# Twelve projections of a hybrid layer as seven products of quarters, in a stage of their own

## The chip, the cores and the metric

The kernel runs on one core of one Trainium2 chip. The metric is the device time of one execution in microseconds (us). The core has a matrix engine (TensorE, PE in the profile, with its weight loads as PEld), three engines for elementwise work (VectorE: DVE, ScalarE: ACT, GpSimd: POOL) and SyncE (SP), which here issues nearly all DMA transfers. Each engine works through its own queue in order and waits on semaphores for the others. On-chip memory (SBUF) has 128 partitions; TensorE writes its results to eight banks of PSUM, each of 512 float32 columns.

## The reference

One decoder layer on 1024 tokens of width 1024, with 256 memory tokens. Cut to what matters here:

```python
h = rmsnorm(x, ln1)
z = h @ w_in                       # one wide projection, split into:
ml_qk, ml_v, ml_o, ml_i, ml_f, fx_q, fx_k, fx_v, fx_f = split(z)
ml_qk = silu(causal_conv(ml_qk, conv_w, conv_b))     # 4 taps along the tokens
mh = mlstm_chunkwise(mq, mk, mv, ml_i, log_sigmoid(ml_f + b))   # 4 heads of 128
ml_out = rmsnorm_per_head(mh) * ml_norm * sigmoid(ml_o)         # ml_o: the output gates
fx_out = forgetting_attention(fx_q, fx_k, fx_v, log_sigmoid(fx_f + b))  # 8 heads of 64
x = x + concat(ml_out, fx_out) @ w_out
x = x + cross_attention(rmsnorm(x), rmsnorm(mem), ...)          # 4 heads of 256
x = x + relu(rmsnorm(x) @ w_ff1) ** 2 @ w_ff2
return rmsnorm(x, ln_f)
```

ml_o (output gates), fx_q (forgetting queries) and fx_k (forgetting keys) are each 512 columns wide, four tiles of 128: twelve tiles that read nothing but h.

## The kernel before

Every float32 matrix product is made of three matmuls. `split` writes a high part (ScalarE, rounded to the matmul's own float32 form) and a low part (the rest, VectorE); `mm3` (lines 190 to 194) multiplies low by high, high by low and high by high into one PSUM bank. `weights` loads a 128x1024 weight tile into one of two raw buffers (wr) and splits it into one of three pairs (wh, wl). `proj` makes a tile of 128 columns for both halves of 512 tokens, with eight contraction tiles: 48 matmuls of 512 columns.

Instructions are written in program order and then put into each engine's queue ahead of time: what is ready goes first, and among the ready the one earlier in the program. So a projection written later can be placed between the steps of a chain written earlier. Where the body stands under `in_order`, the written order is kept on each engine. Buffers are named by tag with a fixed count: act (7 tiles of 128x4096), w4 (5 of 128x1024), z4 (2 of 128x1027), r_a to r_y (one or two of 128x512 each). An allocation waits until a buffer of its tag is free.

The stages in order:

- The inputs arrive, are squared for the norm, scaled by the gain ln1 and split into h (four act tiles: two halves of tokens, high and low). The norm's factor per token is applied to results later: rcol has it by token in columns, row in a row over all partitions.
- `token_major` (line 503) makes values with tokens on the partitions, in matmuls of 256 columns. The first half of the mLSTM values is made while the inputs arrive (`first_values`), the second by `token_major(a["w_mv"], ...)` (line 689). `mv_sink` (line 321) keeps all of them in two act tiles. Between its tiles lie the making of row (`row_first`) and `gate_rows` (line 464): the forget gates' running sums by scans on VectorE.
- `ml_project(hd)` (line 668), for each of four mLSTM heads: `conv_silu` for the key (projection, four taps on VectorE, tanh on ScalarE, split), `fx_project(0, hd)` (a forgetting query tile, scaled, split, stored to DRAM as fqk), `carried` (the state that the first half of tokens hands to the second), `conv_silu` for the query, `fx_project(1, hd)` (a key tile), `carry`, and the output gate's tile. `ml_head(hd)` (line 578) computes the scores, their decay (ScalarE, GpSimd's mask, VectorE), their products with the values, the denominators and the normalized result, in pieces; `closing` is the last piece of a head (or, ahead of head 0, the gate columns and the preparing of the memory tokens), taken up between the steps of the next projection.
- Forgetting attention. `fx_load` reads queries and keys into two stacks, one step of loading per slot (`fx_step`, from a list `coming`). Thirteen slots of scores go ahead (the lead), then `token_major(a["w_fv"], ...)` (line 1090) makes the forgetting values, then 96 slots each transpose, split and multiply a piece of the probabilities. Each slot also gets some filler: units from a list (line 961), first the keys and values of the cross-attention (`key_unit`, `value_unit`, four heads), then the tiles of the output projection over the first five contraction tiles (`out_unit`). `RATE` (line 1101) sets how much filler a slot takes: 3.6, where three matmuls of 512 columns count 3.0. `extra` lists the loads of the operands of `out_unit`.
- The rest of the output projection, cross-attention, and the MLP. The MLP's first product, and most of its second, is made by seven products of quarters in place of eight (`Pair`, line 1393; `left_up`, line 1253, makes the combined weights: four subtractions and additions on GpSimd).

## Time and profile before

| | before |
|---|---|
| time, median of 3 runs | 1513.89 us (1513.47 to 1515.79) |
| profiled execution: span from first to last instruction | 1510.9 us |
| TensorE busy, matmuls | 1498.5 us (99%), 7708 |
| VectorE busy | 1097.5 us (73%) |
| ScalarE busy | 717.5 us (47%) |
| GpSimd busy | 450.6 us (30%) |
| DRAM traffic | 288.33 MB, mean 191 GB/s |
| granted TensorE clock | 0.998 |

For the profiled execution the profile gives its span; the time of an execution also holds what lies before the first and after the last instruction. In a row of the groups of instructions, the line is that of the kernel (often a helper's: L192 to L194 are the three matmuls of `mm3`, L138 and L139 the two parts of a `split`), then engine, operation, result and operands with their shapes and the count; after the bar, busy time, mean of one in ns, and idle time of the engine just before them with what ended it. Names of buffers stand without their numbers, m is the bank m2. Matmuls are pipelined: one starts before the one ahead of it has ended, so that the busy time of a matmul is longer than its distance to the next.

### The profile page before, as it was taken

Reading aid. Unit: us, or ns where it says so; the run is one execution under the profiler, and the core shown is the slowest. Engines: PE = TensorE matmul, PEld = TensorE weight load, DVE = VectorE, ACT = ScalarE, POOL = GpSimd, SP = SyncE. Lnnn points to the kernel's source line nnn. Section 1 sums busy time; section 2 is a strip of 40 time slices with the busy share of each in tenths; the row PEclk is TensorE's granted clock in tenths of the full one; section 3 lists DMA queues with packets and bytes.
Section 4 is the critical chain, followed back from the end, with each engine's and each line's share of the span. In section 5 each row is a group of like instructions: output and inputs, shape, how many; then the busy total and the mean of one; then the engine's idle time right before and its main releaser. Section 6 shows DMA issues by size and latency. Waiting matters only on the chain.

```text
span 1510.9 us, 21868 instructions
## 1 busy us (share of the span) xinstructions
PE 1498.5 (99%) x7708; PEld 1259.5 (83%) x7708; DVE 1097.5 (73%) x1743; ACT 717.5 (47%) x1347; POOL 450.6 (30%) x529
## 2 busy tenths in 40 slices
PE   9999999999999999999999999999999999999997
PEld 8988888889999888888888888888888888888887
DVE  7676676665799875844457988888887788777765
ACT  7343343334788773534444556565656332222134
POOL 0003030413466551001110033344433644343312
PEclk9999999999999999999999999999999999999999
DMA  5332333436889768533334446867766865555623
GB/s 209 117 114 91 115 100 127 129 130 169 279 253 270 218 199 291 198 123 119 119 119 133 154 136 237 281 244 265 272 243 235 352 258 221 223 223 223 251 84 112
DMA packets 114258, 288.33 MB, mean 191 GB/s; under 512 B 12882, under 2 KB 23436, under 8 KB 108516
## 3 DMA queue, kind: packets, MB, share of 16 engines
q1 hardware_dynamic: 113860, 286.83, 56.0%
q8 instruction: 60, 0.98, 0.3%
q14 instruction: 50, 0.41, 0.1%
q10 hardware_dynamic: 288, 0.11, 0.0%
HBM read 194.36 MB, written 92.53 MB: 190 GB/s over the span
## 4 chain that ended last, share of the span: by engine, by line
PE 98%; issue 0%; DVE 0%; DMA 0%; POOL 0%; ACT 0%; POOLq 0%; ACTq 0%; DVEq 0%
PE tp L194 9%; PE tp L193 9%; PE tp L192 9%; PE sc L192 7%; PE sc L194 7%; PE sc L193 7%; PE m L192 6%; PE m L194 6%; PE m L193 6%; PE mm L192 6%; PE mm L193 6%; PE mm L194 6%; PE ov L813 2%; PE ov L192 2%; PE ov L193 2%; PE ov L194 2%
## 5 line engine op out<-in xcount | busy, mean ns | idle before, releaser
L194 PE MATMUL tp<-act,wh 128*128 128x512 f32 (+1 forms) x456 | 178.5, 392 | 0.0
L192 PE MATMUL tp<-act,wl 128*128 128x512 f32 (+1 forms) x456 | 178.5, 392 | 0.0
L193 PE MATMUL tp<-act,wh 128*128 128x512 f32 (+1 forms) x456 | 178.5, 391 | 0.0
L138 ACT ACTIVATE wh<-wr 128x1024 fp32r<-128x1024 f32 (+3 forms) x96 | 92.7, 966 | 95.9 <-PE tp L194 36.6
L139 DVE TENSOR_TENSOR wl<-wr,wh 128x1024 fp32r<-128x1024 f32 (+3 forms) x96 | 113.9, 1187 | 14.5 <-ACT wh L138 14.4
L193 PE MATMUL mm<-act,wh 128*128 128x512 f32 (+1 forms) x320 | 122.6, 383 | 0.0
L192 PE MATMUL mm<-act,wl 128*128 128x512 f32 (+1 forms) x320 | 122.6, 383 | 0.0
L194 PE MATMUL mm<-act,wh 128*128 128x512 f32 (+1 forms) x320 | 122.3, 382 | 0.0
L192 PE MATMUL m<-act,wl 128*128 128x512 f32 (+1 forms) x312 | 119.5, 383 | 0.0
L193 PE MATMUL m<-act,wh 128*128 128x512 f32 (+1 forms) x312 | 118.9, 381 | 0.0
L194 PE MATMUL m<-act,wh 128*128 128x512 f32 (+1 forms) x312 | 118.8, 381 | 0.0
L192 PE MATMUL sc<-act,wl 128*128 128x512 f32 (+1 forms) x268 | 103.8, 387 | 0.0
L193 PE MATMUL sc<-act,wh 128*128 128x512 f32 (+1 forms) x268 | 103.7, 387 | 0.0
L194 PE MATMUL sc<-act,wh 128*128 128x512 f32 (+1 forms) x268 | 103.6, 387 | 0.0
L194 PEld LDWEIGHTS tp<-act,wh 128*128 128x128 f32 x456 | 85.7, 188 | 19.5
L193 PEld LDWEIGHTS tp<-act,wh 128*128 128x128 f32 x456 | 85.8, 188 | 19.0
L192 PEld LDWEIGHTS tp<-act,wl 128*128 128x128 f32 x456 | 85.7, 188 | 19.0
L1491 POOL TENSOR_TENSOR z<-wr 128x256 f32<-128x256 f32 x56 | 50.4, 921 | 147.6 <-DMA wr<-w_ff2q 140.8
L138 ACT ACTIVATE w<-wr 128x768 fp32r<-128x768 f32 (+2 forms) x31 | 25.5, 825 | 133.7 <-PE tp L194 69.2
L138 ACT ACTIVATE wh<-z 128x1024 fp32r<-128x1024 f32 (+2 forms) x55 | 52.5, 956 | 65.0 <-POOL z L1491 28.8
L139 DVE TENSOR_TENSOR wl<-z,wh 128x1024 fp32r<-128x1024 f32 (+2 forms) x55 | 65.9, 1198 | 10.1 <-ACT wh L138 10.1
L194 PEld LDWEIGHTS mm<-act,wh 128*128 128x128 f32 x320 | 60.2, 188 | 12.5
(673 smaller groups left out, 4207.9 us busy)
## 6 DMA issues: line engine op xcount, KB each, us to landing
act<-right SPq DMA_DIRECT2D x35, 1024.0 KB
right<-r_d SPq DMA_DIRECT2D x70, 256.0 KB
right<-w SPq DMA_DIRECT2D x56, 256.0 KB
wr<-w_ff2q SPq DMA_DIRECT2D x28, 512.0 KB
act<-fqk SPq DMA_DIRECT2D x48, 256.0 KB
wr<-w_in SPq DMA_DIRECT2D x20, 512.0 KB
wr<-w_ff SPq DMA_DIRECT2D x20, 512.0 KB
fqk<-r_p SPq DMA_DIRECT2D x32, 256.0 KB
```

The costliest lines, as they stand in the source:

```text
L138: s.activation(hi, src, AF.Copy)
L139: return v.tensor_tensor(out=lo, in0=src, in1=hi.bitcast(F32), op=ALU.subtract)
L192: nc.tensor.matmul(ps, w[1], x[0], start=first, stop=False, skip_group_check=more)
L193: nc.tensor.matmul(ps, w[0], x[1], start=False, stop=False, skip_group_check=more)
L194: nc.tensor.matmul(ps, w[0], x[0], start=False, stop=last, skip_group_check=more)
L813: nc.tensor.matmul(self.ov[:, c0:], self.fv[:, self.j], t[:, c0:], start=self.j == 0 and t is self.p[1], stop=self.last and t is self.p[0])
L1491: g.tensor_tensor(out=o, in0=x, in1=y, op=op)
```

## The change

The twelve tiles leave the heads and get a stage of their own ahead of the heads, between the mLSTM values and `ml_project(0)`. They are joined in six couples: gates 0 and 1, then query and key tile n for n from 0 to 3, then gates 2 and 3. A couple is a product of 256 columns by 1024 contraction by 1024 tokens; each factor is cut into quarters, and seven products of combined quarters give the four quarters of the result.

- The combined quarters of the inputs are made from x scaled by ln1 (VectorE and GpSimd) and split. One of them takes the place of half of h's second half, which is saved to DRAM before (h12d) and read back in the last couple.
- The combined quarters of the weights are made on GpSimd, as in the MLP.
- Partial sums are added by VectorE out of PSUM; ScalarE copies one of seven products.
- Gates go through tanh and to DRAM (ogd); each head reads its own back. Queries and keys go to fqk as before.
- The mLSTM values go to DRAM (mvd) instead of staying in two act tiles; each head reads its own into one tile. The second half of the values is made in the order of tokens 4 to 7, then 0 to 3.
- The weights of `conv_silu` have their low part made by GpSimd, and its first tap is made by ScalarE.
- The forgetting values are made behind heads 0 and 1, one half each. Half of the cross-attention's keys and values (heads 0 and 1) leaves the filler: two key tiles behind head 2, the rest between the lead and the slots of forgetting attention.
- In the slots, a second list (`behind`) is loaded from when `coming` is empty; `RATE` is 3.4.
- The memory tokens are prepared during the new stage.

The core of the diff:

```diff
     def mv_sink(t, c, ps):
-        o = mv[c][:, t].rearrange("p (h e c) -> p h e c", h=2, e=2)
+        o = rotate("d", "e").bitcast(F32R).rearrange("p (h e c) -> p h e c", h=2, e=2)
         split(o[:, :, 0], o[:, :, 1], ps.rearrange("p (h c) -> p h c", h=2), rcol[:, t : t + 1])
+        load(mvd[2 * c : 2 * c + 2, :, t].rearrange("h p c -> p h c"), o.bitcast(F32).rearrange("p h e c -> p h (e c)"))
...
-    steps, cum, rel, run = (t[:GW] for t in quarters())
-    on = w4((GW, T))
+    steps, cum, rel, run = (w4((GW, T)) for _ in range(4))
+    on = z4()[:GW, :T]
...
     def conv_silu(n, hi, lo):
-        w = weights(a["w_in"][n])
+        w = weights(a["w_in"][n], by=g)
...
-        v.tensor_scalar(out=y, in0=z[:, 0:T], scalar1=vec[:, cw : cw + 1], scalar2=..., op0=ALU.mult, op1=ALU.add)
+        s.activation(y, z[:, 0:T], AF.Identity, scale=vec[:, cw : cw + 1], bias=...)
...
     def ml_project(hd):
...
+        mv_load(hd)
         yk = conv_silu(MLH + hd, *k)
         next(closing, None)
-        fx_project(0, hd)
-        next(closing, None)
         state = carried(hd, yk)
         next(closing, None)
         yq = conv_silu(hd, *q)
-        fx_project(1, hd)
-        sums = carry(hd, q, yq, *state)
-        og = w4()
-        for _, hf, ps in proj(weights(a["w_in"][8 + hd]), h, 1):
...
+        next(closing, None)
+        return q, k, *carry(hd, q, yq, *state)
...
+    def first_parts():
+        for e in range(2):
+            cut_part(5, x11, e)
+
+    def third_part():
+        for e in range(2):
+            combine(x12, x11, e, v, x11)
+        for e in range(2):
+            combine(x22, x12, e, g, x12)
+
+    def other_parts():
+        for e in range(2):
+            combine(x22, x11, e, v, x11)
+        for e in range(2):
+            cut_part(6, x11, e)
+        for e in range(2):
+            cut_part(7, x12, e)
...
+    def fourth_part():
+        fourth.extend(w4() for _ in range(2))
+        for e in range(2):
+            combine(x21, x11, e, g, fourth)
...
+    couples = [(gate_sink(0), gate_sink(1))] + [(fx_sink(0, n), fx_sink(1, n)) for n in range(4)] + [(gate_sink(2), gate_sink(3))]
+    NC_ = len(couples)
+    seven_jobs = []
+    for p_ in range(NC_):
+        seven_jobs += [(p_, 1), (p_, 5), (p_, 2)] + ([(p_ - 1, 4)] if p_ else []) + [(p_, 6), (p_, 3), (p_, 7)]
+    seven_jobs.append((NC_ - 1, 4))
...
+        if group == 0:
+            rs = [z4()[:, :1024] if p_ % 2 else sb("wr", [P, 1024], 2) for _ in range(2)]
...
+            for o, x, y, op in ((s3, a11, a21, ALU.subtract), (a21, a21, a22, ALU.add), (a22, a22, s3, ALU.subtract), (a12, a12, a22, ALU.subtract)):
+                g.tensor_tensor(out=o, in0=x, in1=y, op=op)
...
+    def seventh(p_, i):
...
+        if i in (1, 5, 6):
+            u[at_] = bank()
+        ps = u[at_]
+        l, r = lefts_.pop((p_, i)), RIGHT[i]
+        for k in range(4):
+            mm3(ps, both(l, lambda t: t[:, k]), both(r, lambda t: t[:, k]), i in (1, 5, 6) and k == 0, k == 3, True)
...
-    token_major(a["w_mv"], mv_sink, (1,), {2: row_first, 5: gate_rows}, other)
+    token_major(a["w_mv"], mv_sink, (1,), {2: between_2, 4: between_4, 5: gate_rows}, other, (4, 5, 6, 7, 0, 1, 2, 3))
+    turn[0] = 0
+    memory = mem_prepare()
+    for at, (p_, i) in enumerate(seven_jobs):
+        left_ahead(at)
+        if at == 0:
+            other_parts()
+        if at == 2:
+            gate_cols()
+        if at == 3:
+            fourth_part()
+        if at == 5:
+            fourth_cut()
+        if at in (12, 16, 20, 24):
+            next(memory, None)
+        seventh(p_, i)
...
     for hd in range(MLH):
         closing = ml_head(hd, *ready)
         next(closing)
+        if hd < 2:
+            token_major(a["w_fv"], fv_sink, (hd,))
+        if hd == 2:
+            next(extra_work)
         if hd < MLH - 1:
             ready = ml_project(hd + 1)
...
-    for n in range(XH):
+    for n in range(2, XH):
         units += [key_unit(2 * n), value_unit(n), key_unit(2 * n + 1)]
...
-    token_major(a["w_fv"], fv_sink, between={4: lambda: next(closing, None)})
...
+    next(extra_work)
+    next(closing, None)
+    for _ in extra_work:
+        pass
...
-    RATE, DELAY = 3.6, 3
+    RATE, DELAY = 3.4, 3
```

`x11`, `x21` are the lower and upper half of the contraction for the first half of the tokens, `x12`, `x22` for the second. `between_2` makes row and the third combination, `between_4` the cuts of product 5 and the first weights; `left_ahead` makes the weights of a product five products ahead of it.

More of the change, by code (lines that the diff above doesn't have):

```diff
@@ L186, in weight_parts @@
         lo = sb("wl", [P, 1024], 3, F32R)[:, :n]
-        split(hi, lo, raw)
+        split(hi, lo, raw, by=by)
         return hi, lo
@@ new lines, in combine, with cut_part @@
+    def combine(x, y, e, by, out_=None):
+        x, y = (flat2(t, c + 2 * e) for t, c in (x, y))
+        o = flat2(out_[0], out_[1] + 2 * e) if type(out_) is tuple else out_[e]
+        by.tensor_tensor(out=o, in0=x, in1=y, op=ALU.subtract)
+    def cut_part(i, x, e, by=v):
+        if i not in RIGHT:
+            t = act()
+            RIGHT[i] = t[:, lower], t[:, upper]
+        split(*both(RIGHT[i], lambda t: flat2(t, 2 * e)), flat2(x[0], x[1] + 2 * e) if type(x) is tuple else x[e], by=by)
```

258 lines of the change are left out of this document (193 added, 65 removed).

## Prediction

> **What bounds the kernel now.** I read the page first, then the waits of TensorE, then the busy time stage by stage, then the timeline of TensorE inside one projection.
>
> ```profile
> span 1510.9 us, 21868 instructions
> PE 1498.5 (99%) x7708; PEld 1259.5 (83%) x7708; DVE 1097.5 (73%) x1743; ACT 717.5 (47%) x1347; POOL 450.6 (30%) x529
> PE 98%; issue 0%; DVE 0%; DMA 0%; POOL 0%; ACT 0%; POOLq 0%; ACTq 0%; DVEq 0%
> ```
>
> The chain that ended last is TensorE for 98% of the span. The waits of TensorE, longest first, hold nothing else of size:
>
> ```profile
> PE ov L228 <- DVE c_r L220: 1.7, 1, 1.7
> PE mm L192 <- DVE act L142: 1.4, 1, 1.4
> PE ov L118 <- DVE r_y L115: 1.2, 1, 1.2
> ```
>
> No wait is longer than 1.7 us. So a matmul taken out is time taken out, one for one, as long as TensorE always finds another whose operands are there. The stages (columns: stretch, length, busy time with instruction count for PE, PEld, DVE, ACT, POOL, then granted clock, DMA share, GB/s):
>
> ```profile
> 57.00:335.00 278.00, 278.00 (x1362) 231.09 (x1361) 189.43 (x286) 103.24 (x167) 48.53 (x62) 1.00 0.36 113
> 335.00:391.00 56.00, 56.00 (x455) 54.31 (x454) 30.64 (x75) 25.05 (x63) 21.89 (x28) 1.00 0.71 207
> 391.00:545.00 154.00, 152.89 (x1078) 140.19 (x1076) 136.68 (x334) 123.70 (x348) 89.22 (x150) 1.00 0.81 243
> 905.00:1410.00 505.00, 505.00 (x2166) 406.85 (x2165) 403.63 (x489) 230.75 (x338) 207.73 (x175) 1.00 0.69 251
> 57.00:67.00 10.00, 10.00 (x62) 8.48 (x61) 9.96 (x10) 3.16 (x5) 0.00 (x0) 1.00 0.23 61
> ```
>
> The rows are: the mLSTM heads with the projections that are to move (57 to 335), the forgetting values and the lead of the scores (335 to 391), forgetting attention, the MLP's products of quarters, and the ten microseconds in which the gate rows are made. TensorE is full in all of them at clock 1.00.
>
> **What a matmul costs.** The page's mean of about 390 ns for one matmul is not its price, because matmuls overlap. The timeline inside one projection gives the pitch:
>
> ```profile
> 59.84 0.40 PE L192 MATMUL tp<-act,wl 128*128 128x512 f32 x1
> ...
> 65.20 0.40 PE L194 MATMUL tp<-act,wh 128*128 128x512 f32 x1
> ...
> 330.28 0.28 PE L192 MATMUL tp<-wh,act 128*128 128x256 f32 x1
> ...
> 333.11 0.28 PE L192 MATMUL mm<-wh,act 128*128 128x256 f32 x1
> ```
>
> From 59.84 to 65.20 lie 23 steps: 0.233 us for 512 columns. From 330.28 to 333.11 lie 24 steps of 256 columns: 0.118 us.
>
> **The products removed.** Before, each of the twelve moved column tiles (four output gates, four query and four key tiles) takes two halves of eight contraction tiles with three matmuls: 48, in all 576. After, each of six couples takes seven products of four contraction tiles with three matmuls: 84, in all 504. 72 matmuls of 512 columns go: 72 x 0.233 = 16.8 us. (With the mean of 392 ns in the group's row below it would be 28 us, which is the trap of this profile.) The Trainium skill, "TensorE: Matmul & The Clock Gate", section "Back-to-back issue gap", gives columns / 2.4 + 2.5 ns; by it a matmul of 512 columns would cost 0.216 us and the saving would be 15.5 us. The trace's 0.233 decides.
>
> ```profile
> L194 PE MATMUL tp<-act,wh 128*128 128x512 f32 (+1 forms) x456 | 178.5, 392 | 0.0
> ```
>
> The forgetting values, the mLSTM projections and the cross-attention keys and values keep their matmuls; they only change place. TensorE's own work falls by 16.8 us and by nothing else.
>
> **The steady run of the new stage.** A couple lasts 84 x 0.233 = 19.6 us of TensorE. VectorE's and GpSimd's rows for its pieces:
>
> ```profile
> L139 DVE TENSOR_TENSOR wl<-wr,wh 128x1024 fp32r<-128x1024 f32 x22 | 26.7, 1215 | 0.0
> L653 DVE SCALAR_TENSOR_TENSOR r_p<-tp,row 128x512 f32<-128x512 f32 x8 | 5.5, 686 | 4.8 <-DMA fqk<-r_p 3.5 <-PE tp L194 1.3
> L139 DVE TENSOR_TENSOR r_p<-r_p,r_p 128x512 fp32r<-128x512 f32 x16 | 12.1, 755 | 3.4 <-ACT r_p L138 3.2
> L1234 POOL TENSOR_TENSOR r_e<-z,z 128x512 f32<-128x512 f32 x7 | 10.8, 1540 | 134.5 <-DMA z<-w_ff 131.4 <-DVE w L1234 3.0
> L1273 POOL TENSOR_TENSOR wr<-wr 128x512 f32<-128x512 f32 x7 | 13.7, 1962 | 0.5
> ```
>
> VectorE per couple: weight splits of 3.5 tiles of 1024 columns, 4.3 us; five additions out of PSUM and four scalings by the token factor, 9 x 0.69 = 6.2; four low parts, 3.0: 13.5 of 19.6 us. GpSimd: four combinations of weights, near 4 x 1.7 = 6.8 us. The MLP stage already runs this scheme with VectorE at 403.6 of 505 us (80%) and GpSimd at 41%, and TensorE loses nothing there; the new stage asks 69% and 35%. I cost the steady run at nothing; were its cover gone, VectorE would set the pace only from 19.6 us per couple.
>
> DRAM carries more: mLSTM values, gates and a saved half of the inputs go out and back, some 16.8 MB (4.2, 2.1 and 2.1 MB, each twice). Spread over 57 to 335 that adds 60 GB/s to the 113 of its row, 173 in all; forgetting attention runs at 243 with TensorE full. SyncE's queue gets the stores of values and gates ahead of later weight loads; a store waits for its sink there, and the weights behind it wait too. The MLP stage queues its stores and loads the same way without loss, so nothing, with 3 us as the bad end.
>
> **The start of the new stage.** Here buffers and VectorE decide. The first couple needs four combined quarters of the inputs. Quarter product 5 is cut into the old second half as soon as the reordered value projection has left it, product 6 goes into the one free activation buffer. Product 7 needs an eighth: it must wait until the fourth combination (GpSimd) has read the first input tile. That combination writes two w4 tiles, and of the five, four hold the gate rows until these are done; the row 57 to 67 shows VectorE at 9.96 of 10 us with just that work (67 us). Then two halves on GpSimd at about 2 x 1.54 each (6 us) and the two cuts, 1.2 us each with ScalarE's part ahead (4 us): about 77 to 79 us. Product 7 is sixth in line, due at 57 + 5 x 2.8 = 71 us. Until then three products of the second couple can pass (8.4 us), if their weights are in. The second couple's raw weights want both z4 buffers, one of which holds the row of ones until the gate rows are done. So the term lies between 0 and 11 us; I take 4, since part of the late supply is passed over.
>
> **The heads without their company.** Before, the head stage mixes the 576 matmuls (134 us) among the heads' own chains. After, heads 0 and 1 get the forgetting values instead (384 x 0.118 = 45.3 us), head 2 two key tiles (5.7 us), the end the other three pieces (17 us). VectorE is relieved as well: the splits of the conv weights go to GpSimd and the first conv tap to ScalarE.
>
> ```profile
> L683 DVE TENSOR_TENSOR w<-tp,row 128x512 f32<-128x512 f32 x4 | 2.7, 684 | 0.0
> L142 DVE SCALAR_TENSOR_TENSOR r_c<-tp,rcol,r_c 128x256 fp32r<-128x256 f32 x3 | 1.5, 484 | 5.5 <-ACT r_c L141 5.5
> L475 DVE TENSOR_TENSOR_SCAN act<-w,act 12x1024 f32<-12x1024 f32 x1 | 2.3, 2278 | 2.3 <-ACT act L470 2.3
> L142 DVE SCALAR_TENSOR_TENSOR w<-act,w 12x1024 fp32r<-12x1024 f32 x2 | 2.4, 1208 | 0.7 <-DMA decay<-w 0.7
> L761 DVE TENSOR_REDUCE c_mx<-sc 128x1 f32<-128x512 f32 x5 | 3.4, 683 | 0.3 <-PE sc L734 0.3
> L525 DVE TENSOR_SCALAR z<-z,vec 128x1024 f32<-128x1024 f32 x8 | 7.2, 906 | 0.2
> L527 DVE SCALAR_TENSOR_TENSOR z<-z,vec,z 128x1024 f32<-128x1024 f32 x24 | 32.3, 1345 | 0.2
> L530 DVE SCALAR_TENSOR_TENSOR z<-z,z 128x1024 f32<-128x1024 f32 x8 | 10.2, 1280 | 1.9 <-ACT z L529 1.9
> L529 ACT ACTIVATE z<-z 128x1024 f32<-128x1024 f32 x8 | 8.5, 1060 | 23.7 <-DVE z L527 23.7
> L994 POOL TENSOR_TENSOR wl<-wr,wh 128x256 fp32r<-128x256 f32 x32 | 26.4, 846 | 5.2 <-ACT wh L988 3.7 <-issue 1.3 <-POOL act L778 0.2
> ```
>
> VectorE from 57 to 391 has 189.4 + 30.6 = 220 us. Out go the weight splits 26.7, L653's 16 operations at 0.69 (11), their low parts 12.1, the gates' 8 at L683's 0.68 (5.5), the taps 7.2: 62 us. The gate rows and decays (two scans, four smaller operations, two decays: 10 to 12) stay with the start. Taking off the values' sinks (16 x 0.48 and four splits, 12.6) and the lead's maxima (13 of at most 0.68, 8 with their small ones), the four heads keep about 125, 31 each. TensorE in the same stretch: 334 - 134 - 45 - 6 for the lead's scores - 3 for the end of the values projection = 146, 36 per head. So heads 0 and 1 stay rich in TensorE work (36 + 22.7 against 31 + 6). The tail, heads 2 and 3 with the three pieces and the lead, has 73 + 22.7 + 6 = 102 us of TensorE against 62 + 15 + 8 = 85 us of VectorE (15: eight weight splits and four keys' and four values' small ones), with perhaps 10 more left over from head 1: 83% to 93%. The nearest row is forgetting attention, VectorE at 136.7 of 154 us (89%), where TensorE is idle for 1.1 us; but that stretch has its order written out and small pieces to fill with, and the tail has neither after the last projection. The conv weights' low parts on GpSimd (four times 0.85 us, so about 3 us a tile against 1.2) are loaded a tile ahead and cost nothing unless they queue behind a head's masks. Bounds 0 to 21 us (the upper end is the third rival); I take 5.
>
> **The attention.** The filler rate falls from 3.6 to 3.4 and half the key and value tiles are done before it, so output tiles begin some 22 slots earlier. Their fifth operand (the first forgetting heads) is asked for behind the other loads, close to its use: nothing, with one late load of 3 us as the bad end; the 1.1 us of idle may go too.
>
> **The sum.** The profiled execution is given by its span of 1510.9 us; the median of the three times is 1513.89, so 3.0 us lie around the span, and I leave them. 1513.9 - 16.8 + 4 + 5 = 1506.1.
>
> **The rivals.** First, no new wait: the queues are laid so that TensorE always has something ready, as everywhere before. For it: each stage's row shows TensorE full. Against it: 72 matmuls fewer to hide the same chains. Stalls below 4 us give 1497 to 1501, with 1498 likeliest.
>
> Second, a late start in one piece: product 7 and the second couple's weights come late together, 11 us, and the tail loses 7; 1513.9 - 16.8 + 18 = 1515, no change that can be told. A long gap may also slow TensorE itself:
>
> ```profile
> 1.24 4.46 PE L118 MATMUL ov<-r_y 128*128 128x512 bf16 x11 [1.24 <-DVE r_y L115]
> ```
>
> These first eleven matmuls after idleness took 0.405 us each, 1.9 us more than eleven at 0.233. A gap as long as that would add 1.9. The Trainium skill, "TensorE: Matmul & The Clock Gate", section "What's actually happening", says that about 3.4 us of idleness halves the clock until as long a busy window; no gap here before is that long (1.7 at most, clock 1.00), so the trace can't confirm it, only agree with the slow beginning.
>
> Third, on the other side: heads in series. In heads 2 and 3, after the query projection, VectorE's chain is 0.69 + 1.06 + 3 x 1.345 + 1.06 + 1.28 and the split 1.06 + 1.2: 10.4 us, before any score can be computed. If TensorE waits it out twice, that is 21 us, with the start 1513.9 - 16.8 + 4 + 21 = 1522. It decides when the next key projection (48 x 0.233 = 11.2 us) is queued behind the scores instead of ahead of them, or its weights wait for buffers; with stalls of 20 us in all the change is slower. Before, TensorE's order mixes projections among the score matmuls, which speaks against.
>
> **Chances.** Forecast (stalls 4 to 13 us, 1501 to 1510) 0.45; no new wait 0.25; late start 0.16; heads in series 0.14. A difference of 0.2%, 3 us, is what can be told from no change. A quarter of the second rival still lies below 1510.9, so faster 0.74, the same 0.12, slower 0.14. The range 1497 to 1516 leaves out the third rival and little else; its lower end is the first rival's.
>
> **What would show it.** Right: 7636 matmuls; TensorE's busy time near 1482; waits of TensorE of a few microseconds on the combined quarters between 65 and 85 us; others on the conv or score operands between about 240 and 330; the couples 19.6 us apart. The forecast is wrong if couples are longer than 20 us (VectorE or GpSimd sets the pace), if forgetting attention gets waits that it had not, or if waits of TensorE sum to over 20 us.

## The result, and the profile after

The changed kernel takes 1622.45 us (median of 4 runs, 1621.49 to 1624.22) against 1513.68 (4 runs of the kernel before, 1513.23 to 1515.79): ratio 1.072, 95% interval 1.071 to 1.074. It is slower by 108.8 us; forecast was faster by 8.

The page of the changed kernel: span, the engines' busy time, and the first line of the chain that ended last.

```profile
span 1620.9 us, 21939 instructions
PE 1527.6 (94%) x7636; PEld 1273.2 (79%) x7636; DVE 1154.7 (71%) x1787; ACT 755.7 (47%) x1395; POOL 505.2 (31%) x549
PE 55%; DMA 2%; DVE 0%; issue 0%; SPq 0%; ACT 0%; POOLq 0%; POOL 0%; DVEq 0%; ACTq 0%
```

The 72 matmuls are gone (7636 left), but TensorE is busy for 94% of a longer span where it had been 99%, and it is busy 29 us *longer* with fewer matmuls: it waited, and it ran slow. The third line does not show that. Its shares add up to 57% of the span because this chain is followed back only to 682 us, behind the start, the heads and the tail, and TensorE holds 55 of the 57; the 98% of before can't be set beside it. TensorE's waits, longest first (columns: in total, times, longest):

```profile
PE mm L192 <- DVE r_f L576: 9.0, 1, 9.0
PE tp L192 <- DVE wl L139: 8.3, 2, 5.5
PE mm L550 <- DVE r_b L547: 8.0, 1, 8.0
...
PE m L193 <- DMA act<-mix: 2.4, 1, 2.4
```

Here r_f is a head's carried numerator, wl the low part of a weight tile, r_b the key row, and act<-mix an operand of the output projection that arrives by DMA. Before, the longest wait was 1.7 us. By stages (columns as in the prediction: length, PE, PEld, DVE, ACT, POOL, clock, DMA share, GB/s):

```profile
0.00:150.00 150.00, 122.36 (x680) 104.16 (x681) 107.76 (x154) 77.26 (x130) 42.88 (x34) 0.91 0.47 159
150.00:235.00 85.00, 85.00 (x370) 68.53 (x369) 55.73 (x75) 27.05 (x40) 18.92 (x11) 1.00 0.61 209
235.00:460.00 225.00, 195.37 (x1177) 172.85 (x1175) 138.64 (x217) 90.17 (x148) 64.18 (x69) 0.95 0.45 132
460.00:511.00 51.00, 29.52 (x129) 24.24 (x129) 28.03 (x67) 20.58 (x52) 14.09 (x22) 0.66 0.28 97
511.00:1620.00 1109.00, 1095.35 (x5283) 903.41 (x5283) 824.56 (x1277) 540.61 (x1027) 365.08 (x413) 0.99 0.60 206
```

These are the start with the first couples, the steady run of the new stage, the heads, the tail behind the last query projection, and the rest. The steady run is full at clock 1.00. Start, heads and tail are not, and no other engine is full there either: VectorE has 72%, 62% and 55%. That points to chains of steps and not to one engine's load; the experiments test it.

**An account of the loss.** I cut the span at two matmuls that both kernels have: the first transpose of the first head's key row (L545 before, L550 after) and the first transpose of forgetting attention (L793, L1019). Before, then after:

```profile
87.76 0.60 PE L545 MATMUL ov<-ident,r_b 128*128 128x128 f32 x4
...
390.85 0.27 PE L793 MATMUL tp<-ident,w 128*128 128x128 f32 x1
```

```profile
L550 PE MATMUL ov<-ident,r_b x4: 272/272/273, 240.6 to 241.0; 128*128 128x128 f32 x4
```

```profile
511.46 0.41 PE L1019 MATMUL tp<-ident,w 128*128 128x128 f32 x1
```

To the first key row, six couples (6 x 19.6 = 117.6) should make 87.8 into 205.4; it is 240.6, so the **start** loses 35.3 us. From there to attention 576 matmuls went (134.4) and 22.7 us of key and value tiles came; 303.1 should become 191.4 and is 270.8, so **heads and tail** lose 79.5. The **rest** lost its 22.7 and should take 1097.4 us; it takes 1109.4, a loss of 12.1. 35.3 + 79.5 + 12.1 - 16.8 is the span's +110 (rounded); it must be, since each loss is what the span has above its expected part. I use "lost" in this sense for each run below.

**The clock.** The same 126.8 us in another cut: TensorE's idle time rose from 12.4 to 93.3 us (span less busy time), which is 81; the other 46 are matmuls that took longer (1527.6 busy, where 1498.5 - 16.8 would do). Most of the 46 is the clock: by the trace's record of it, TensorE was busy for 74.6 us at half rate (1.0 before), and half of that, 37 us, is the price. I estimate the rest from the rows: the last matmul ahead of a gap counts with its whole 0.39 us, and not with the pitch of 0.233, and there are some 50 gaps more than before. TensorE behind the wait at 97 us (start, duration, in brackets the idle time before it and what ended it):

```profile
102.91 0.79 PE L192 MATMUL tp<-act,wl 128*128 128x512 f32 x1 [5.49 <-DVE wl L139]
...
107.27 0.39 PE L193 MATMUL tp<-act,wh 128*128 128x512 f32 x1
```

Ten matmuls in 4.36 us, 0.43 apart, where 0.233 is the pitch: the gap of 5.5 us costs 2.0 more. The prediction had 1.9 for a gap of that kind, and the rule that it cited (the Trainium skill, "TensorE: Matmul & The Clock Gate", section "What's actually happening": half rate after an idle window of about 3.4 us, until as long a busy one) agrees with this row; the last section shows a shorter gap that does not fit it as simply. In the tail the granted clock is 0.66 on the mean.

### The profile page after: what moved, and what is told of

Read it like the earlier page. It is cut to its first block, busy times and chain, and to the rows that moved or that the text cites. A ratio compares the mean times of both kernels' runs of the same rounds, so it can differ in the third digit from the quotient of the medians.

```text
span 1620.9 us, 21939 instructions
## 1 busy us (share of the span) xinstructions
PE 1527.6 (94%) x7636; PEld 1273.2 (79%) x7636; DVE 1154.7 (71%) x1787; ACT 755.7 (47%) x1395; POOL 505.2 (31%) x549
## 4 chain that ended last, share of the span: by engine, by line
PE 55%; DMA 2%; DVE 0%; issue 0%; SPq 0%; ACT 0%; POOLq 0%; POOL 0%; DVEq 0%; ACTq 0%
PE sc L192 5%; PE sc L193 5%; PE sc L194 5%; PE tp L192 5%; PE tp L193 5%; PE tp L194 5%; PE m L192 3%; PE m L193 3%; PE m L194 3%; PE mm L192 3%; PE mm L193 3%; PE mm L194 3%; PE ov L192 2%; PE ov L193 2%; PE ov L194 2%; DMA act<-mix 1%
## 5 line engine op out<-in xcount | busy, mean ns | idle before, releaser
L192 PE MATMUL tp<-act,wl 128*128 128x512 f32 (+1 forms) x416 | 163.4, 394 | 8.4 <-DVE wl L139 8.3
L193 PE MATMUL tp<-act,wh 128*128 128x512 f32 (+1 forms) x416 | 162.9, 392 | 0.2 <-DMA act<-mix 0.2
L194 PE MATMUL tp<-act,wh 128*128 128x512 f32 (+1 forms) x416 | 162.4, 391 | 0.0
L192 PE MATMUL sc<-act,wl 128*128 128x512 f32 (+1 forms) x316 | 123.7, 392 | 4.3 <-DVE wl L139 4.3
L193 PE MATMUL sc<-act,wh 128*128 128x512 f32 (+1 forms) x316 | 123.7, 391 | 1.6 <-DVE act L139 1.6
L194 PE MATMUL sc<-act,wh 128*128 128x512 f32 (+1 forms) x316 | 123.6, 391 | 0.0
L192 PE MATMUL mm<-act,wl 128*128 128x512 f32 (+1 forms) x280 | 108.3, 387 | 11.4 <-DVE r_f L576 9.0
L193 PE MATMUL m<-act,wh 128*128 128x512 f32 (+1 forms) x280 | 108.6, 388 | 2.4 <-DMA act<-mix 2.4
L194 PE MATMUL m<-act,wh 128*128 128x512 f32 (+1 forms) x280 | 108.1, 386 | 0.0
L193 PE MATMUL mm<-act,wh 128*128 128x512 f32 (+1 forms) x280 | 107.4, 384 | 0.0
L194 PE MATMUL mm<-act,wh 128*128 128x512 f32 (+1 forms) x280 | 107.2, 383 | 0.0
L138 ACT ACTIVATE wh<-z 128x1024 fp32r<-128x1024 f32 (+2 forms) x64 | 60.7, 950 | 79.5 <-POOL z L1714 30.1
L193 PEld LDWEIGHTS tp<-act,wh 128*128 128x128 f32 x416 | 79.8, 192 | 17.4 <-DMA act<-mix 0.6
L194 PEld LDWEIGHTS tp<-act,wh 128*128 128x128 f32 x416 | 79.6, 191 | 17.5
L139 DVE TENSOR_TENSOR wl<-z,wh 128x1024 fp32r<-128x1024 f32 (+2 forms) x64 | 77.8, 1216 | 15.4 <-ACT wh L138 15.3
L192 PEld LDWEIGHTS sc<-act,wl 128*128 128x128 f32 x316 | 59.9, 190 | 18.4 <-DVE wl L139 4.8
```

What stands on the lines that cost most here:

```text
L138: s.activation(hi, src, AF.Copy)
L139: return by.tensor_tensor(out=lo, in0=src, in1=hi.bitcast(F32), op=ALU.subtract)
L192: nc.tensor.matmul(ps, w[1], x[0], start=first, stop=False, skip_group_check=more)
L193: nc.tensor.matmul(ps, w[0], x[1], start=False, stop=False, skip_group_check=more)
L194: nc.tensor.matmul(ps, w[0], x[0], start=False, stop=last, skip_group_check=more)
```

## The experiments

My theory: in three places the removed projections, or other independent work, had covered chains of steps that run through several in-order engines (theory 1). The rival: the change loads VectorE and GpSimd more, and they set the pace (theory 2). Times of one run each, unless said otherwise; each stood beside a run of the kernel before, at 1513.0 to 1514.2. Four runs of the changed kernel lie 2.7 us apart, so a smaller difference between single runs shows nothing.

**The heads by themselves** (no_twelve). The kernel *before* without the twelve projections:

```diff
-        w = weights(a["w_in"][12 + 4 * which + n])
-        for _, hf, ps in proj(w, h, 1):
...
+        for hf in range(2):
+            for p_ in range(2):
+                load(fqk[which, p_, n, :, hf * TH : hf * TH + TH], row[:, hf * TH : hf * TH + TH])
...
-        for _, hf, ps in proj(weights(a["w_in"][8 + hd]), h, 1):
...
+        g.memset(og, 0.0)
```

> The kernel before, with the twelve projections left out (no weights, matmuls and sinks; gates are zeros, and forgetting queries and keys are the token factors, so the output is another one). 576 matmuls of 0.233 us go, 134 us. Theory 1: the heads alone cannot keep TensorE busy, so of the 134 us only 60 to 90 are gained: 1425 to 1455, with waits of several us on the key row of the carried state behind the factors' way through DRAM. Theory 2: VectorE has 50 us less to do in the heads, so TensorE stays full and the time is 1380 to 1390.

1456.4 us: of 134 us of TensorE work only 57.8 came off. No new stage, no values through DRAM, no work moved to GpSimd, and between key row and attention it still loses 75.8 us. Its longest waits of TensorE and its head stage:

```profile
PE sc L192 <- DVE r_b L599: 12.6, 2, 6.6
PE m L192 <- DVE r_f L571: 5.8, 1, 5.8
```

```profile
110.00:333.00 223.00, 187.30 (x1030) 162.06 (x1028) 138.66 (x249) 82.78 (x162) 63.69 (x83) 0.86 0.35 104
```

VectorE has 62% there. This is just above theory 1's range (by 1.4 us) and far from the rival's.

**The cover put back** (cover_back). The converse: the changed kernel computes the eight query and key projections a second time, at their old places.

```diff
         next(closing, None)
+        fx_project(0, hd)
         state = carried(hd, yk)
         next(closing, None)
         yq = conv_silu(hd, *q)
+        fx_project(1, hd)
```

> Changed kernel with more work: the eight projections of forgetting queries and keys are computed a second time in the heads, at the places where they stood before, and go to a scratch tile in DRAM that nobody reads. It adds 384 matmuls of 0.233 us, 89.6 us of TensorE work. Theory 1 (a head has more waiting in it than TensorE has work, and the projections filled that): the first five of them are nearly free, the granted clock rises to 0.98 or more, and the run comes to 1650 to 1685 us, 28 to 63 us above the changed kernel. Rival (the waits in the heads come from the change's own additions, values from DRAM, cuts on GpSimd, and stay whatever stands beside): 1700 to 1720 us.

1654.0 us, within theory 1's range: 89.6 us of work cost 31.5. The head stage, which had 195 busy of 225 us:

```profile
235.00:500.00 265.00, 262.17 (x1494) 227.94 (x1492) 153.42 (x239) 95.20 (x152) 60.05 (x67) 1.00 0.43 135
```

262 of 265 busy at clock 1.00; the one wait of TensorE left there is 1.0 us long. Heads and tail lose 22.8 us in place of 79.5. These two runs settle the larger part: a head needs its company.

**VectorE's relief taken back** (ve_back).

```diff
-        w = weights(a["w_in"][n], by=g)
+        w = weights(a["w_in"][n])
...
-        s.activation(y, z[:, 0:T], AF.Identity, scale=vec[:, cw : cw + 1], bias=...)
+        v.tensor_scalar(out=y, in0=z[:, 0:T], scalar1=vec[:, cw : cw + 1], scalar2=..., op0=ALU.mult, op1=ALU.add)
```

> The low part of the conv weights and the first conv tap go back to VectorE (17 us of VectorE work more in the heads, some 24 of GpSimd less). Theory 1: latencies, not loads, so within 5 us of 1622. Theory 2, VectorE's load: 10 to 17 us slower, 1632 to 1640; theory 2, GpSimd's load: 5 to 15 us faster.

1623.8, 1.4 us more. VectorE got its conv splits and taps back, GpSimd lost its share, and nothing followed: VectorE was busy for 7.7 us more and GpSimd for 18.4 less, and heads and tail lose 81.7 in place of 79.5. For the heads theory 2 falls. The run does not touch the load that the change puts on the two engines in the start.

**Only the gates in the stage** (gates_only): queries and keys stay in the heads, forgetting values behind the lead.

```diff
-    couples = [(gate_sink(0), gate_sink(1))] + [(fx_sink(0, n), fx_sink(1, n)) for n in range(4)] + [(gate_sink(2), gate_sink(3))]
+    couples = [(gate_sink(0), gate_sink(1)), (gate_sink(2), gate_sink(3))]
...
+        fx_project(0, hd)
...
+        fx_project(1, hd)
```

> Only the four output gates in the stage of seven products (two couples); the eight projections of forgetting queries and keys stand in the heads again, where they were before, the forgetting values behind the lead, the cross-attention's keys and values all in the slots. The start is that of the changed kernel. Theory 1 (the heads lose because they lost their projections as cover): the heads and the tail lose next to nothing, the start its 37 us, 24 matmuls of 0.233 us are saved: 1540 to 1560 us. Rival (the heads are slowed by what the change put into them, values read back from DRAM and weights cut by GpSimd, whatever projections stand beside): the heads still lose 30 us or more, 1575 to 1590 us.

1558.3, within theory 1's range: the start loses 31.1 (35.3 in the whole change), heads and tail 17.4 in place of 79.5, the rest 2.8. The 17.4 are more than theory 1's "next to nothing"; the gates' projections are still missing in these heads, but that this is the reason was not tested.

**What binds the heads.** VectorE of the changed kernel around the wait at 298 us (start, duration; in brackets the idle time before it):

```profile
299.52 1.23 DVE L535 SCALAR_TENSOR_TENSOR z<-z,z 128x1024 f32<-128x1024 f32 x1 [1.18 <-ACT z L534]
304.21 0.75 DVE L647 SCALAR_TENSOR_TENSOR r_f<-r_f,vec,r_a 128x512 f32<-128x512 f32 x1 [3.47 <-DMA r_a<-facd]
304.88 0.68 DVE L547 SCALAR_TENSOR_TENSOR r_b<-z,r_b 128x512 f32<-128x512 f32 x1
```

The key row L547 is ready to go at 300.7 but stands behind L647, the closing of the head before, which waits for the factors' way through DRAM (transposed at 297.5, back at 304.2). So I tried to start that way earlier (close_early):

```diff
-            token_major(a["w_fv"], fv_sink, (hd,))
+            token_major(a["w_fv"], fv_sink, (hd,), {t: early_closing for t in (2, 5, 7)})
...
-        yk = conv_silu(MLH + hd, *k)
+        yk = conv_silu(MLH + hd, *k, lambda: next(closing, None))
```

> Changed kernel, with the closing steps of an mLSTM head issued earlier: behind heads 0 and 1 within the forgetting values (ahead of tiles 2, 5 and 7), behind head 2 after the first half of the next head's key projection, so that the factors' round trip through DRAM has begun before the key row of the carried state stands on VectorE. Theory 1 (in the heads, what lost its cover is above all this round trip, which stands on VectorE ahead of the next head's rows): the gaps of 7.95 us at 298 and 9.04 us at 460 shrink below 3 us, and with the slow matmuls behind them the run comes to 1600 to 1612 us. Rival (the chain projection, convolution, key row, scores is serial in itself, and the closing merely stands where TensorE would wait anyway): the gaps keep their places with other names, and the run stays within 4 us of 1622.

1620.9, as the rival has it: gaps of 7.6 and 8.0 us where 7.95 and 9.0 had been. The factors themselves (L634 there) were ready at 298.3 only; TensorE had used up forgetting values and projections as filler between the scores by 299, so the end of a head again came when nothing else was left. Next, room for the rows that tie two heads together, the one r_a and the two r_f, in a free act tile (head_room, on fv_back, below):

```diff
-        num, den = w2("f"), w2("b")
+        num, den = slot_of("num", 2 * (hd % 2)), w2("b")
...
-            nmb = w2("a")
+            nmb = slot_of("nmb", hf)
...
-            fb = fbs[hf] or w2("a")
+            fb = fbs[hf] if end else slot_of("fb", hf)
```

> The run fv_back (1609.2 us) with room for the heads' rows: the row of each half (formerly the one buffer r_a), the factors' row (the same buffer) and the four numerators (the two buffers r_f) of two heads get slices of a free act tile. Nothing else changes. Theory 1a (two heads are tied together by these buffers: the next head's rows wait for the closing of the head before, and this for the factors' round trip through DRAM): the distances of the heads' key rows, 41.2, 53.3 and 58.4 us in fv_back, fall to 36 to 46 us, and the run comes to 1575 to 1595 us. Rival (the chain within a head is what lasts; the buffers only show where it ends): distances within 4 us of these, 1603 to 1615 us.

1596.9, 12.3 less and just above the expected range: heads and tail lose 65.5 where fv_back loses 74.8. The distances of the key rows split the verdict: 41.1 and 51.3 us stay as the rival has it, and only the third falls, from 58.4 to 48.4. And with both closings behind the next head's numerator, plus the later scalings of late_scale, below (head_late):

> The run head_room with both closing steps of a head behind the next head's query projection and carried numerator, which the room now allows, and with the scalings of x behind the input cuts as in late_scale (which alone gave 13 us). Theory 1a: VectorE no longer stands at the closing with the key row behind it, the gaps over 4 us in the heads are gone, 1560 to 1580 us. Rival (the gaps move to the next link of the chain): within 5 us of head_room less 13.

1582.2, as the rival has it: of 14.7 us all but 2 are late_scale's. Key rows of fv_back, then of head_late (starts in us):

```profile
L550 PE MATMUL ov<-ident,r_b x4: 272/272/273, 241.7 to 242.0; 128*128 128x128 f32 x4
...
L550 PE MATMUL mm<-ident,r_b x4: 272/273/274, 282.8 to 283.8; 128*128 128x128 f32 x4
...
L550 PE MATMUL tp<-ident,r_b x4: 421/421/476, 336.1 to 336.8; 128*128 128x128 f32 x4
...
L550 PE MATMUL m<-ident,r_b x4: 272/272/305, 394.5 to 394.8; 128*128 128x128 f32 x4
```

```profile
L550 PE MATMUL ov<-ident,r_b x4: 272/272/273, 228.8 to 229.1; 128*128 128x128 f32 x4
...
L550 PE MATMUL mm<-ident,r_b x4: 271/272/273, 267.5 to 268.5; 128*128 128x128 f32 x4
...
L550 PE MATMUL tp<-ident,r_b x4: 421/421/477, 319.6 to 320.3; 128*128 128x128 f32 x4
...
L550 PE MATMUL m<-ident,r_b x4: 272/273/330, 366.9 to 367.3; 128*128 128x128 f32 x4
```

41.1, 53.3 and 58.4 us from head to head became 38.7, 52.1 and 47.3. The prediction had 36 us of TensorE work for a head; a head without company takes up to 52 even with free buffers. I read that rest as the head's own chain (projection, convolution, scores, masks, sums, factors); no run here broke it, and how its links share the time is not shown.

**The tail** (fv_back). Forgetting values behind the lead again, all key and value tiles in the slots, rate 3.6:

```diff
-        if hd < 2:
-            token_major(a["w_fv"], fv_sink, (hd,))
-        if hd == 2:
-            next(extra_work)
...
+    token_major(a["w_fv"], fv_sink, between={4: lambda: next(closing, None)})
```

> The new stage and the heads as in the changed kernel, but the forgetting values stand behind the lead again and all keys and values of the cross-attention are filler again, with the rate and the loads of before. Theory 1: the tail between the last head and the first value slot loses under 5 us instead of 34, and the heads, with no values and no key tiles between them, lose 10 to 30 us more than their 45; in all 1595 to 1625, with the loss moved from the tail to heads 0 and 1. Theory 2: the work of each engine is unchanged, so the losses of heads and tail stay where they are, and the time within 5 us of 1622.

1609.2, within theory 1's range. The rest now loses 2.3 us in place of 12.1: so the loss in attention (the late `act<-mix` operand of the waits, and a slow beginning) came with the new order of loads and fillers. Heads and tail lose 74.8 in place of 79.5, but elsewhere. The heads, then what follows the last wait of 7.0 us at the end of the last head:

```profile
242.00:425.00 183.00, 151.80 (x695) 125.49 (x693) 118.95 (x180) 70.48 (x115) 54.21 (x61) 0.85 0.29 88
440.00:485.00 45.00, 44.65 (x358) 42.64 (x357) 26.94 (x67) 22.89 (x58) 17.22 (x22) 1.00 0.77 228
```

What follows is full at clock 1.00, where the changed kernel has 28.5 of 41 us (470 to 511) at 0.67. The heads without the values are idle for 31 us at 0.85, where they were idle for 30 (241 to 455) at 0.94. The 45 us of values cover one place or the other, and there is not enough for both. With its heads left alone this run is also the closest to no_twelve: 74.8 us lost here, 75.8 there, without any of the change's additions. So these add next to nothing to the loss of heads and tail.

**The start.** First ScalarE's sixteen scalings of x, which the change queues among the cuts of the inputs (late_scale):

```diff
+            with tc.issue_after(begun):
-            s.activation(t[:, k], t[:, k], AF.Copy, scale=...)
+                s.activation(t[:, k], t[:, k], AF.Copy, scale=...)
```

> The sixteen scalings of x by ln1 are queued on ScalarE behind the last activation of the input stage. Theory 1 (chains that lost their cover, one of them at the start, where the scalings stand among the input cuts and push the token factors back): the first token factors come at about 30 us and the second at about 42 instead of 34 and 51, TensorE's loss up to 72 us falls from 18 to about 8, and the whole is 8 to 12 us shorter, 1610 to 1615. Theory 2 (the added work of VectorE and GpSimd is the bound): the work is the same, so the time stays within 3 us of 1622.

1609.5 (-13.0), just below theory 1's range; the start loses 22.4 in place of 35.3. Then two buffers more (start_free):

```diff
-    on = z4()[:GW, :T]
-    g.memset(on, 1.0)
+    on = ones[:GW, 0:1].broadcast_to([GW, T])
...
-        neg = on
+        neg = run
...
-            s3 = s3s[p_] = w2("e")
+            s3 = s3s[p_] = w2("e" if p_ else "f")
```

> Changed kernel with three repairs of its start: the scalings of x by ln1 behind the input cuts (as in the run late_scale), the row of ones of the gate rows replaced by a broadcast column and its negative made in place (so that the second couple's raw weights find their z4 buffers free), and the first couple's difference in buffer f in place of e (which waits for the mLSTM values' stores). Theory 1 (the start loses its 37 us to these three waits and to the slow clock behind each): 1590 to 1603 us, and the gaps of 3.6 us at 63 and 5.5 us at 97 are gone. Rival (the scalings were all; the other two waits hide each other or other waits that end at the same time): 1606 to 1612 us.

1615.6, above both ranges: start 21.3, only 1.1 better than late_scale, and the heads lost 7.7 more, with a new wait of 8.6 us at 387 for ScalarE's half of a convolution's split (L141). The memory tokens out of the stage (mem_back; they become the `closing` of the first head's projections):

> Changed kernel with the memory tokens prepared beside the first head's projections, as before, in place of beside the new stage; nothing else changes. In the changed kernel ScalarE stands 14.4 us (longest 7.7) for the memory tokens' loads between 30 and 150 us, and cuts of the next weights are queued behind. Theory 1b (these loads are what TensorE waits for at 97 and 135 us, 5.5 and 4.3 us, through ScalarE's queue): the first head's key row comes at 226 to 233 us in place of 240.6, the run at 1605 to 1616 us unless the heads lose it again. Rival (the weights were late by z4's buffers and the gate rows): the key row at 238 us or later.

1620.2, key row at 237.4, start 32.0: close to the rival. The wait for the second couple's weights tells why. In mem_back, in start_free, and in start_all, which has both repairs and one of GpSimd's queue:

```profile
PE tp L192 <- DVE wl L139: 5.5, 1, 5.5
```

```profile
PE tp L192 <- DVE wl L139: 6.0, 1, 6.0
```

```profile
PE tp L192 <- DVE wl L139: 2.4, 1, 2.4
```

ScalarE splits these weights ahead of VectorE. What it waited for on the way to them, in mem_back and in start_free:

```profile
96.44 0.63 ACT L138 ACTIVATE r_b<-z 128x512 fp32r<-128x512 f32 x1 [4.44 <-DMA z<-w_in]
```

```profile
104.01 0.63 ACT L298 ACTIVATE w<-w 128x512 f32<-128x512 f32 x1 [4.77 <-DMA w<-mem]
```

Two causes stood side by side: the raw weights, late because the row of ones held their z4 buffer, and the memory tokens' loads ahead of the split on ScalarE's queue. With either repaired alone the other kept the wait whole. In start_all neither wait is there, and 2.4 us are left; what its third repair gave of that was not tested alone. start_all:

```diff
+        with tc.issue_after(guesses[1].ins):
+            for e in range(2):
+                combine(x22, x12, e, g, x12)
...
+        with tc.issue_after(guesses[1].ins):
+            left_ahead(-4)
```

> The run start_free (key row of the first head at 226.6 us) with two more repairs: the memory tokens prepared in the first head, and GpSimd's combinations for the first couple queued behind the guess of the second token factors, so that this small operation does not stand behind them in GpSimd's queue and VectorE's three small operations after it do not run beside them (2.35, 1.18 and 2.26 us for 128x4 in start_free, 0.16 us before). Theory 1b (the start loses its time to a handful of in-order queues, each repairable): the gaps at 45 us (6.9) and 104 us (6.0) are gone, the key row at 207 to 216 us. Rival (a repaired wait uncovers the next of the same size, since the chain of x's combinations and first weights is too long for the work before it): 222 us or later.

1611.1; the key row at 221.7, start 16.3: between the two ranges, close to the rival's. Heads and tail lose 89.2, 8.8 more than in late_scale, so that the run is no faster than late_scale. The gap at 45 us stayed (6.1). VectorE of start_all there, and GpSimd beside it:

```profile
44.43 3.20 DVE L139 TENSOR_TENSOR wl<-wr,wh 128x1024 fp32r<-128x1024 f32 x1 [2.88 <-ACT wh L138]
47.56 1.75 DVE L139 TENSOR_TENSOR r_c<-wr,r_b 128x512 fp32r<-128x512 f32 x1
49.23 2.82 DVE L139 TENSOR_TENSOR r_c<-z,r_b 128x512 fp32r<-128x512 f32 x1
51.97 0.47 DVE L142 SCALAR_TENSOR_TENSOR r_d<-sc,rcol,r_d 128x256 fp32r<-128x256 f32 x1
```

```profile
44.14 2.41 POOL L694 TENSOR_TENSOR act<-act 128x1024 f32<-128x1024 f32 x1
...
48.72 2.79 POOL L694 TENSOR_TENSOR act<-act 128x1024 f32<-128x1024 f32 x1
```

The values' sink (L142), for whose bank TensorE waits, stands behind three cuts that take 1.2 and 0.7 us elsewhere and 1.8 to 3.2 here, beside GpSimd: in the start theory 2 holds in this part. 16 us of the start stay unexplained in detail.

**Do the repairs add?** The start of start_free and gates_only together (gates_free); then all repairs (all_repairs, with the memory tokens between stage and heads), and once more with these back in the stage (add_up, 4 runs).

> The run gates_only with the three repairs of the start from start_free. Theory 1: the sum of both, 1505 to 1530 us. Rival (the repairs only move the wait to the next thing that is late): 1535 us or more.

> All repairs together: those of start_all (the memory tokens here between the new stage and the first head, on ScalarE behind the stage), and those of head_late (room for the heads' rows, closings behind the next head's numerator, forgetting values behind the lead). Theory 1: the gains add, 1555 to 1572 us, still over 40 us above the kernel before, since the heads keep the chain that the projections covered. Rival (the gains share the same cover and do not add): 1575 us or more.

> The run all_repairs with the memory tokens where the change has them, beside the new stage: all_repairs lost 10.4 us in one wait for their factors ahead of the first head, which was that placement's own. So this is head_late (1582.2 us) with the buffer and queue repairs of the start. Theory 1 (repairs of the start and of the heads add): the first key row at 222 to 225 us in place of 228.8, 1574 to 1579 us. Rival (they draw on the same cover; what the start gives, the heads lose): 1580 us or more. Either way it stays over 55 us above the kernel before.

They don't; each time it is as the rival has it. gates_free takes 1561.6, 3.3 *more* than gates_only: the start gained 7.4 and the heads lost 11.1. all_repairs takes 1592.9: its memory tokens made a wait of 10.4 us of their own. add_up takes 1581.7 (1580.8 to 1582.2), 1.045 times the kernel before (1.043 to 1.047). That can't be told from head_late's 1582.2: the start is 2.2 better, the heads 1.1 and the rest 0.9 worse. Why the heads give back what the start gains stays open. No version that does the whole work beats the kernel before.

The account of the main runs, in us lost (of cover_back and gates_only against what their own work should take):

| run | time | start | heads and tail | rest |
|---|---|---|---|---|
| changed kernel | 1622.45 | 35.3 | 79.5 | 12.1 |
| no_twelve | 1456.36 | 0.9 | 75.8 | 1.4 |
| cover_back | 1653.97 | 35.6 | 22.8 | 10.2 |
| gates_only | 1558.29 | 31.1 | 17.4 | 2.8 |
| fv_back | 1609.17 | 36.3 | 74.8 | 2.3 |
| late_scale | 1609.47 | 22.4 | 80.4 | 10.8 |
| head_late | 1582.20 | 23.4 | 62.7 | 0.4 |
| start_all | 1611.14 | 16.3 | 89.2 | 9.8 |
| add_up | 1581.68 | 21.2 | 63.8 | 1.3 |

## Why the prediction was wrong

- **The products removed**: right. 7636 matmuls are left, and where TensorE is not kept waiting the pitch is 0.233, so the -16.8 stands.
- **The steady run**: right. Full at clock 1.00 with VectorE at 66% (forecast 69%).
- **The heads without their company** is the step that failed: "Bounds 0 to 21 us ... I take 5", measured 79.5. I set TensorE's load against VectorE's, head by head, found room (83% to 93%), and took the step as hidden. But an engine at 62% can still be the one that is waited for, if its operations stand in a row. The question was how long a head takes from its first step to its last with nothing beside it; the trace of before could not show it, since the company was there, but it could have been summed, as I did for one link only: the 10.4 us of conv chain in the third rival. That rival had the right kind, heads in series, the right side and a quarter of the size (21 us); it counted two waits of one link, and the closing, the factors and the clock were not in it. Its chance of 0.14 was too small.
- **The start**: forecast 4, bounds 0 to 11, measured 35.3. The places named were partly right: the weights of the second couple were late, and TensorE stood still for them for 5.5 us up to 102.9, by the row of ones and by a load that I had not looked at. The largest single term, 13 us, was not in the sum: a moved or added instruction counts on its own queue too, and ScalarE's sixteen scalings (about 10 us, at 0.63 each) stood ahead of the cuts and token factors.
- **Attention**: forecast nothing, with a late operand of 3 us as the bad end. It was that operand (waits of 2.4 and 0.7 us), and with the slow matmuls behind it and a slow beginning (clock 0.92 from 511 to 545) 12.1.
- **The clock** was priced rightly for one gap and put into one rival only. It is about 37 of 126.8 us: every long gap of the sum should have carried it.
- The marks "waits of TensorE sum to over 20 us" and "attention gets waits that it had not" were the ones that showed the forecast wrong; "couples longer than 20 us" was not.

## What to carry to other kernels

Before independent work is taken out of a stage, add up the stage's chain with nothing beside it, through every engine and DRAM trip, and compare *that* with TensorE's remaining work; shares of busy time can't answer it. A saving on the engine that is full is worth its price only while something else is ready to run, and a long gap is paid twice, once as idleness and once at half clock (81 and about 37 us here). And when a repaired wait stays as long as it was, look for a second cause beside it before giving up the first.

## What the runs showed of the hardware

- VectorE can stand still while GpSimd works. In start_free, three operations on 4 columns, and the combinations that GpSimd ran meanwhile:

```profile
43.55 2.35 DVE L218 TENSOR_TENSOR c_t<-c_y 128x4 f32<-128x4 f32 x1 [4.79 <-POOL c_y L213]
45.94 1.18 DVE L219 SCALAR_TENSOR_TENSOR c_t<-c_t,c_var 128x4 f32<-128x4 f32 x1
47.16 2.26 DVE L220 SCALAR_TENSOR_TENSOR rcol<-c_t,c_y 128x4 f32<-128x4 f32 x1
```

```profile
43.48 2.40 POOL L692 TENSOR_TENSOR act<-act 128x1024 f32<-128x1024 f32 x1
45.83 1.27 POOL L793 TENSOR_TENSOR wr<-wr 128x512 f32<-128x512 f32 x1
47.05 2.35 POOL L692 TENSOR_TENSOR act<-act 128x1024 f32<-128x1024 f32 x1
```

  Each ends within 0.02 us of the GpSimd operation beside it; before, the same three took 0.15 to 0.16 us. The Trainium skill, "GPSIMD Engine Reference", section "1. Specifications", calls GpSimd's SBUF interfaces shared with VectorE, with contention where VectorE has two SBUF inputs; these three have, and the rows agree.
- The clock can fall behind a gap shorter than 3.4 us, and with a delay. Behind 2.0 us of idleness TensorE of the changed kernel first went on at full rate:

```profile
327.51 0.39 PE L192 MATMUL m<-wh,act 128*128 128x256 f32 x1 [2.01 <-DVE r_p L142]
...
329.22 0.41 PE L193 MATMUL m<-wl,act 128*128 128x256 f32 x1
329.43 0.41 PE L194 MATMUL m<-wh,act 128*128 128x256 f32 x1
```

  From 329.2 the steps are 0.21 us in place of 0.118. Behind 2.72 us at 245.7 nothing of the kind followed. The trace's record of the clock tells the two apart. In it the clock changes only at the ends of stretches of 3.41 us that lie one behind the other, wherever the gaps are. Two such stretches in a row at each of the two places (columns as before: PE second, clock third from the end):

```profile
325.63:329.05 3.42, 1.54 (x13) 1.54 (x14) 3.14 (x4) 2.21 (x4) 0.31 (x2) 1.00 0.19 54
329.05:332.46 3.41, 3.41 (x17) 3.22 (x16) 0.95 (x3) 0.47 (x1) 0.51 (x1) 0.50 0.12 28
243.71:247.13 3.42, 1.96 (x17) 1.76 (x15) 3.35 (x3) 0.28 (x1) 0.71 (x1) 1.00 0.51 153
247.13:250.54 3.41, 2.15 (x18) 2.15 (x19) 2.42 (x4) 1.88 (x3) 0.00 (x0) 1.00 0.24 84
```

  The gap of 2.01 us lies almost whole in one stretch, which is busy for 45%, and the next runs at half rate. The gap of 2.72 us is shared by two, busy for 57% and 63%, and the clock stays. Over the traces of all 17 kernels here, each of the 124 stretches at full rate in which TensorE had matmuls for under 40% of the time was followed by half rate, and none of the more than 6400 with over 90%; between these both occur, and what decides there stays open.
